# Projection v as seven quarter products, with the block sums of h built from the transposes

## Chip, core and metric

One Trainium2 chip, one of its cores. The metric is the device time of one execution in microseconds (us); the median of three executions is given. The engines run their own queues in order: TensorE (PE in the profile; its weight loads are PEld), VectorE (DVE), ScalarE (ACT), GpSimd (POOL) and SyncE (SP), which here issues the DMAs.

## What is computed

One residual block over 1024 positions of 1024 channels, all in float32:

```python
h    = rmsnorm(x, norm_g)
proj = h @ w_in                     # 1024 x 9216: u, v, z, x_b, c_b, b_b, z_b, g_a, g_b
v    = rmsnorm(gelu(v), v_norm_g)
s    = gelu(u) * (tril(w_s) v + b)  # in chunks of 128 positions
y_a  = s * silu(z)
y_b  = b_b * conv3(c_b * x_b) * silu(z_b)
m    = sigmoid(g_a) * (y_a @ P_a) + sigmoid(g_b) * (y_b @ P_b)
out  = rmsnorm(x + m @ w_out, final_norm_g)
```

The case is about the first part: the norm of x and the projection v, 1024 of the 9216 columns.

## The kernel before

Every float32 product is made of three TensorE matmuls on rounded halves (`mm`, L76): with a = a_hi + a_lo and b likewise, a_hi b_hi + a_lo b_hi + a_hi b_lo. `split` (L72) makes the halves: ACT casts the high one, DVE subtracts it from the source. x is loaded in eight tiles of 128 positions, its squares summed on ACT, the root taken on POOL (`rsqrt_mean`, L60), the tile scaled on DVE, and turned by eight TensorE transposes into two PSUM banks (`transpose_x`, L111). So h lies in four quarters `B[kh][th]` (half kh of the channels, half th of the positions), high and low; DVE copies it once more into `hst`, and it is written to `h_d` in device memory.

All later projections are made in seven quarter products instead of eight (`step`, L331): with B11, B21, B22 the quarters and T1 = B12 - B11, T2 = B22 - T1, T3 = B22 - B12, T4 = B21 - T2, and like sums S1 to S4 of the weight quarters (`weights`, L302). The T blocks are made by `h_blocks` (L272), which reads the quarters back from `h_d` and splits the differences. Projection v alone, the first one, is a plain product: loop L216 makes its left 512 columns, tile by tile as x arrives (`pv0`, 8 x 8 x 3 matmuls of 512 columns), loop L288 its right 512 columns (`pv1`, the same number), with `h_blocks` queued inside it. `v_out` (L129) takes a PSUM bank through Gelu and a square on ACT and writes the tile to `v_d`.

Order: inside `manual_schedule` the named engines keep the order of the code (L142: all five; L215: SP, ACT, DVE); elsewhere a planner orders the instructions. Space: 20 buffers of 8 KB a partition (`big`), ten of 4 KB (`page`: halves of weights, tiles of v), two for raw weights (`rawt`), eight PSUM banks. An allocation waits until a buffer of its kind is free. After v the first step is `pbc0` (`proj("bc", 0)`, L398).

## Time and profile before

| | us |
|---|---|
| median of three executions | 989.87 |
| lowest, highest | 987.47, 991.25 |
| the profiled execution | 991.29 |
| its span, first to last instruction | 989.6 |

Times of rows count from the span's start. An instruction's row has its start, its length, its engine and line, what it writes and reads, and in brackets the idle time ahead of it with what ended it. Matmuls are pipelined: a row of 0.39 us is followed by the next before it ends, so the distance of starts is the cost.

### The profile page before, as it was taken

How to read it: one execution, taken by the hardware profiler on the slowest of the kernel's cores; microseconds unless marked ns; L12 is line 12 of the kernel's file. 1: busy time of each engine (PE TensorE's matmuls, PEld its weight loads, DVE VectorE, ACT ScalarE, POOL GpSimd, SP SyncE). 2: the span in 40 equal slices, each digit the busy share in tenths (PEclk: the TensorE clock that was granted, in tenths of full speed). 3: DMA queues.
4: the chain of work that ended last, by engine and by line, in shares of the span. 5: the costliest groups of instructions: out<-in, count | busy, mean ns of one | idle time of the engine just before them, and what ended most of it. 6: DMA issues, size and time to landing. Idle time of an engine off the chain costs nothing.

```text
span 989.6 us, 10913 instructions
## 1 busy us (share of the span) xinstructions
PE 963.7 (97%) x4310; PEld 796.7 (81%) x4310; DVE 658.4 (67%) x746; ACT 406.4 (41%) x544; POOL 32.3 (3%) x73
## 2 busy tenths in 40 slices
...
GB/s 241 187 144 188 202 144 44 43 137 67 43 117 85 43 118 79 92 154 50 187 98 117 117 86 215 343 338 326 323 243 302 291 286 243 212 373 49 123 106 107
DMA packets 129113, 164.83 MB, mean 167 GB/s; under 512 B 4229, under 2 KB 87205, under 8 KB 125478
## 3 DMA queue, kind: packets, MB, share of 16 engines
...
q10 hardware_dynamic: 576, 1.05, 0.3%
...
q14 instruction: 18, 0.15, 0.0%
...
## 4 chain that ended last, share of the span: by engine, by line
PE 87%; DMA 7%; DVE 2%; ACT 2%; issue 1%; SPq 0%; POOL 0%; POOLq 0%; ACTq 0%; DVEq 0%
PE pbc_x L79 5%; PE pu_x L79 4%; PE pga_x L79 4%; PE pbz_x L79 4%; PE ox L79 4%; PE ax L79 4%; PE pgb_x L79 4%; PE pz_x L79 4%; PE pbb_x L79 4%; PE pbx_x L79 4%; PE bx L79 4%; DMA h<-h_d 3%; PE be L79 2%; PE pbc_e L79 2%; PE oe L79 2%; PE ae L79 2%
## 5 line engine op out<-in xcount | busy, mean ns | idle before, releaser
L79 PE MATMUL pv<-wv_hi,h_hi 128*128 128x512 f32 x120 | 48.2, 402 | 5.6 <-ACT h_hi L73 5.1
L79 PE MATMUL pv<-wv_hi,h_lo 128*128 128x512 f32 x120 | 47.3, 397 | 0.6 <-DVE h_lo L74 0.6
L79 PE MATMUL pv<-wv_lo,h_hi 128*128 128x512 f32 x120 | 47.2, 394 | 0.0
L79 PEld LDWEIGHTS pv<-wv_hi,h_hi 128*128 128x128 f32 x120 | 22.9, 191 | 11.2 <-ACT h_hi L73 5.5
L74 DVE TENSOR_TENSOR yaP_lo<-yaP,yaP_hi 128x1024 fp32r<-128x1024 f32 x14 | 16.9, 1220 | 22.5 <-ACT yaP_hi L73 22.5
L79 PEld LDWEIGHTS pv<-wv_hi,h_lo 128*128 128x128 f32 x120 | 22.9, 191 | 5.6 <-DVE h_lo L74 1.1
L79 PEld LDWEIGHTS pv<-wv_lo,h_hi 128*128 128x128 f32 x120 | 22.9, 191 | 4.9 <-DVE wv_lo L74 0.3
L270 DVE TENSOR_TENSOR h<-h,h 128x1024 f32<-128x1024 f32 x8 | 9.4, 1221 | 21.9 <-DMA h<-h_d 21.9
L338 DVE TENSOR_TENSOR pbz<-pbz_z,pbz 128x512 f32<-128x512 f32 x4 | 2.8, 691 | 28.6 <-PE pbz_z L79 28.6
L74 DVE TENSOR_TENSOR h_lo<-xp,h_hi 128x512 fp32r<-128x512 f32 x16 | 11.0, 685 | 14.5 <-ACT h_hi L73 14.4
L406 DVE SCALAR_TENSOR_TENSOR pbx<-pbc,cwT,pbx 128x1023 f32<-128x1023 f32 (+1 forms) x16 | 20.1, 1276 | 0.0
L74 DVE TENSOR_TENSOR ybP_lo<-ybP,ybP_hi 128x1024 fp32r<-128x1024 f32 x14 | 16.8, 1217 | 4.0 <-ACT ybP_hi L73 4.0
L338 DVE TENSOR_TENSOR pz<-pz_z,pz 128x512 f32<-128x512 f32 x4 | 2.8, 691 | 24.9 <-PE pz_z L79 24.9
L338 DVE TENSOR_TENSOR pbx<-pbx_z,pbx 128x512 f32<-128x512 f32 x4 | 2.8, 692 | 24.9 <-PE pbx_z L79 24.9
L74 DVE TENSOR_TENSOR wv_lo<-wv_raw,wv_hi 128x1024 fp32r<-128x1024 f32 x4 | 4.9, 1223 | 20.1 <-ACT wv_hi L73 20.1
L65 POOL TENSOR_SCALAR ro<-oss4a 128x1 f32<-128x1 f32 x1 | 0.2, 191 | 537.8 <-ACT osq4a L603 537.8
L131 ACT ACTIVATE v<-pv 128x512 f32<-128x512 f32 x16 | 9.5, 596 | 16.8 <-PE pv L79 10.8
L73 ACT CAST yoP_hi<-mt 128x1024 fp32r<-128x1024 f32 x6 | 6.3, 1053 | 22.4 <-DVE mt L270 22.4
L448 PEld LDWEIGHTS pm<-cst,va 128*128 128x128 f32 x128 | 14.9, 192 | 0.3
L448 PE MATMUL pm<-cst,va 128*128 128x128 f32 x128 | 14.9, 275 | 0.0
L73 ACT CAST T_hi<-h 128x1024 fp32r<-128x1024 f32 x8 | 8.4, 1047 | 15.0 <-DVE h L270 14.8
L79 PE MATMUL pbc_x<-h_hi,pbc_ahi 128*128 128x512 f32 x16 | 7.3, 459 | 7.3 <-ACT pbc_ahi L73 7.3
...
## 6 DMA issues: line engine op xcount, KB each, us to landing
...
```

What stands on the lines that cost most here:

```text
L65: nc.gpsimd.tensor_scalar(u, ss, 1.0 / D, t, ALU.mult, ALU.add)
L73: nc.scalar.copy(hi, src)
L74: nc.vector.tensor_tensor(lo, src, hi.bitcast(F32), ALU.subtract)
L79: nc.tensor.matmul(acc, a[i], b[j], start=start and n == 0, stop=stop and n == 2, skip_group_check=not check)
L131: nc.scalar.activation(vt, pv, AF.Gelu)
L270: nc.vector.tensor_tensor(out_[:, js, :], a[:, js, :], b[:, js, :], op)
L338: add = lambda o, a: nc.vector.tensor_tensor(o, a, o, ALU.add)
L406: nc.vector.scalar_tensor_tensor(xx[:, b, t:], c[:, b, :S - t], col(2 - t), xx[:, b, t:], ALU.mult, ALU.add)
L448: nc.tensor.matmul(pm[:, n * P:(n + 1) * P], v[:, b, h * HP + n], wsT[:, gg_ * P:(gg_ + 1) * P], start=True, stop=True)
```

## The change

v becomes seven quarter products P1 to P7 like the other projections, with positions in the role that columns had: A11, A12, A21, A22 are the quarters of its weights (A12 is the lower left, A21 the upper right). P1 = B11 A11 starts as x arrives, tile by tile of 128 positions; P2 = B21 A12 and P5 = T1 S1 follow in the same written order, which now holds all five engines until P5's last matmul. P6, P7, P3 and P4 stand behind it in the planner's part. The results of P1, P6, P7 and P4 add up in four banks `vx`, those of P5 and P3 in four banks `ve`, P2's are added on DVE from `vz`.

`h_d` is gone. `keep` copies the transposes of the first four tiles out of PSUM on ACT, `diff` subtracts these copies from the transposes of the last four on DVE, which gives T1 and T2 as the tiles come; T3 and T4 are one more difference each of what is kept. The B12 quarter has no halves of its own any more. All of x and of v's weights is asked for at the start; A22 is loaded a second time later, since S1 and S2 are made in its place on POOL. The weights of `pbc0` are loaded and split before P4 (`early`), in `big` buffers. The new functions and the order (what is removed stands in the listing above):

```diff
-    B = [[tuple(block4(big(f"h{kh}{th}_{n}", F32R)) for n in ("hi", "lo")) for th in range(2)]
-         for kh in range(2)]
-    h_d = dram("h_d", [P, KT, S])
...
+    BLOCKS = ["B11", "B21", "B22", "T1", "T2", "T4", "T3"]
+    T, raw_h = {}, {}
+    def new_block(n):
+        T[n] = tuple(block4(big(f"{n}_{m}", F32R)) for m in ("hi", "lo"))
...
+    def square_x(i):
...
+        nc.scalar.activation(sq, xs[i], AF.Square, accum_out=ss)
+        rx[i] = rsqrt_mean([ss], f"rx{i}")
+    def norm_x(i):
+        nc.vector.scalar_tensor_tensor(xs[i], xs[i], rx[i], g_bc, ALU.mult, ALU.mult)
...
+    def block_of(i, kh):
+        return ("B11", "B21")[kh] if i < 4 else ("T1", "B22")[kh]
+    def cols(t, i):
+        return t[:, :, i % 4 * P:(i % 4 + 1) * P]
...
+    def transposes(i, kh):
+        n = block_of(i, kh)
+        if i % 4 == 0:
+            new_block(n)
+            n = {"B22": "T2"}.get(n, n)
+            raw_h[n] = block4(big(f"{n}_raw"))
+        p = psum(f"xp{i}_{kh}")
+        for k in range(HP):
+            nc.tensor.transpose(p[:, k * P:(k + 1) * P], xs[i][:, (kh * HP + k) * P:(kh * HP + k + 1) * P], ident)
+        pt[i, kh] = block4(p)
+    def part_src(i, kh):
+        return cols(raw_h["T1"], i) if (i >= 4, kh) == (True, 0) else pt[i, kh]
+    def high(i, kh):
+        nc.scalar.copy(cols(T[block_of(i, kh)][0], i), part_src(i, kh))
+    def low(i, kh):
+        hi, lo = T[block_of(i, kh)]
+        tt(cols(lo, i), part_src(i, kh), cols(hi, i).bitcast(F32), ALU.subtract)
+    def keep(i, kh):
+        nc.scalar.copy(cols(raw_h[block_of(i, kh)], i), pt[i, kh])
+    def diff(i, kh):
+        a, b = (("T1", "B11"), ("T2", "T1"))[kh]
+        tt(cols(raw_h[a], i), pt[i, kh], cols(raw_h[b], i), ALU.subtract)
...
-        for j in range(1, 4):
-            start_rows(j)
+        start_rows(1)
         for i in (2, 3):
             nc.sync.dma_start(xs[i], x[0, i * P:(i + 1) * P, :])
+        for j in (2, 3):
+            start_rows(j)
...
+        for i in (4, 5):
+            xs.append(load_x(i))
+        w_raw = {"A11": raws[0], "A12": raws[1]}
+        def v_raw(n, kh):
+            w_raw[n] = block4(big(f"wv_{n}"))
+            for j in range(2):
+                rows = wv[(kh * HP + 2 * j) * P:(kh * HP + 2 * j + 2) * P, D + NH:2 * D]
+                nc.sync.dma_start(w_raw[n][:, 2 * j:2 * j + 2, :], rows.rearrange("(j p) e -> p j e", p=P))
+        v_raw("A21", 0)
+        for i in (6, 7):
+            xs.append(load_x(i))
+        v_raw("A22", 1)
+        def v_mm(bank, w, t, m, start=True):
+            for k in range(HP):
+                mm(bank, [h[:, k, m * P:(m + 1) * P] for h in T[t]], w[k], start and k == 0, k == HP - 1, start)
+        def v_hi(n, j):
+            hi, lo = (page(f"wv{n}{j}_{m}", F32R).rearrange("p (j e) -> p j e", j=2) for m in ("hi", "lo"))
+            nc.scalar.copy(hi, w_raw[n][:, 2 * j:2 * j + 2, :])
+            return hi, lo
+        def v_lo(n, j, hi, lo, eng=nc.vector):
+            eng.tensor_tensor(lo, w_raw[n][:, 2 * j:2 * j + 2, :], hi.bitcast(F32), ALU.subtract)
+            return [(hi[:, k, :], lo[:, k, :]) for k in range(2)]
+        def v_parts(n):
+            return [w for j in range(2) for w in v_lo(n, j, *v_hi(n, j))]
+        vx, vz, ve, vq = [], [], [], {"C11": block4(big("vC11"))}
+        def p1(m):
+            vx.append(psum(f"vx{m}"))
+            v_mm(vx[m], w0, "B11", m)
+        def p2(m):
+            vz.append(psum(f"vz{m}"))
+            v_mm(vz[m], w2, "B21", m)
+        def p5(m):
+            ve.append(psum(f"ve{m}"))
+            v_mm(ve[m], ws1, "T1", m)
+        def snap(q, m, bank):
+            nc.scalar.copy(vq[q][:, m, :], bank)
+        def add(q, m, bank):
+            o = vq[q][:, m, :]
+            tt(o, bank, o, ALU.add)
+        def first_norm(i, r, h):
+            cs = halves[h]
+            nc.vector.scalar_tensor_tensor(xs[i][:, cs], xs[i][:, cs], r, pg[h], ALU.mult, ALU.mult)
...
         r0 = rsqrt_mean(ss0, "rx0")
-        for h, cs in enumerate(halves):
-            nc.vector.scalar_tensor_tensor(xs[0][:, cs], xs[0][:, cs], r0, pg[h], ALU.mult, ALU.mult)
+        first_norm(0, r0, 0)
+        first_norm(0, r0, 1)
         w0 += start_split(0, nc.gpsimd)
...
+        square_x(1)
+        transposes(0, 0)
+        high(0, 0)
+        low(0, 0)
...
         w0 += start_split(1, nc.gpsimd)
...
+        vx.append(psum("vx0"))
+        for b, a, k in [(0, 0, 0), (0, 0, 1), (0, 1, 0), (0, 1, 1), (1, 0, 0), (1, 0, 1)]:
+            nc.tensor.matmul(vx[0], T["B11"][a][:, k, :P], w0[k][b], start=a + b + k == 0, stop=False)
+        square_x(2)
+        keep(0, 0)
+        transposes(1, 0)
+        high(1, 0)
+        for b, a, k in [(0, 0, 2), (0, 0, 3), (0, 1, 2), (0, 1, 3), (1, 0, 2), (1, 0, 3)]:
+            nc.tensor.matmul(vx[0], T["B11"][a][:, k, :P], w0[k][b], start=False, stop=(b, k) == (1, 3))
         for h, cs in enumerate(halves):
             nc.vector.tensor_copy(g_bc[:, cs], pg[h])
...
+        norm_x(2)
+        low(1, 0)
+        square_x(3)
+        snap("C11", 0, vx[0])
+        transposes(2, 0)
+        high(2, 0)
+        keep(1, 0)
+        norm_x(3)
+        low(2, 0)
+        p1(1)
+        w2 = [v_hi("A12", 0)]
+        square_x(4)
+        w2[0] = v_lo("A12", 0, *w2[0], nc.gpsimd)
+        transposes(3, 0)
+        snap("C11", 1, vx[1])
+        high(3, 0)
+        keep(2, 0)
+        p1(2)
+        w2.append(v_hi("A12", 1))
+        low(3, 0)
+        norm_x(4)
+        w2 = w2[0] + v_lo("A12", 1, *w2[1])
+        transposes(0, 1)
+        high(0, 1)
+        low(0, 1)
+        square_x(5)
+        snap("C11", 2, vx[2])
+        keep(3, 0)
+        p1(3)
+        transposes(1, 1)
+        high(1, 1)
+        keep(0, 1)
+        low(1, 1)
+        norm_x(5)
+        square_x(6)
+        p2(0)
+        snap("C11", 3, vx[3])
+        transposes(2, 1)
+        transposes(4, 0)
+        high(2, 1)
+        keep(1, 1)
+        low(2, 1)
+        diff(4, 0)
+        high(4, 0)
+        s1 = w_raw["S1"] = w_raw["A22"]
+        nc.gpsimd.tensor_tensor(s1[:, :2], w_raw["A21"][:, :2], s1[:, :2], ALU.add)
+        square_x(7)
+        nc.gpsimd.tensor_tensor(s1[:, 2:], w_raw["A21"][:, 2:], s1[:, 2:], ALU.add)
+        add("C11", 0, vz[0])
+        norm_x(6)
+        p2(1)
+        transposes(3, 1)
+        transposes(5, 0)
+        high(3, 1)
+        ws1 = [v_hi("S1", j) for j in range(2)]
+        ws1 = [w for j in range(2) for w in v_lo("S1", j, *ws1[j], nc.gpsimd)]
+        keep(2, 1)
+        low(3, 1)
+        diff(5, 0)
+        low(4, 0)
+        high(5, 0)
+        add("C11", 1, vz[1])
+        norm_x(7)
+        p2(2)
+        transposes(6, 0)
+        keep(3, 1)
+        low(5, 0)
+        diff(6, 0)
+        high(6, 0)
+        add("C11", 2, vz[2])
+        p2(3)
+        transposes(7, 0)
+        low(6, 0)
+        diff(7, 0)
+        high(7, 0)
+        add("C11", 3, vz[3])
+        low(7, 0)
+        transposes(4, 1)
+        high(4, 1)
+        p5(0)
+        low(4, 1)
+        diff(4, 1)
+        transposes(5, 1)
+        high(5, 1)
+        transposes(6, 1)
+        high(6, 1)
+        p5(1)
+        for i in (5, 6):
+            low(i, 1)
+            diff(i, 1)
+        w_raw["S2"] = s1
+        for j in range(2):
+            nc.gpsimd.tensor_tensor(s1[:, 2 * j:2 * j + 2], s1[:, 2 * j:2 * j + 2],
+                                    w_raw["A11"][:, 2 * j:2 * j + 2], ALU.subtract)
+        transposes(7, 1)
+        high(7, 1)
+        low(7, 1)
+        diff(7, 1)
+        new_block("T2")
+        ws2 = []
+        for j in range(2):
+            js = slice(2 * j, 2 * j + 2)
+            split(*(t[:, js, :] for t in T["T2"]), raw_h["T2"][:, js, :])
+            ws2 += v_lo("S2", j, *v_hi("S2", j))
+        for js in (slice(0, 2), slice(2, 4)):
+            tt(w_raw["A21"][:, js], w_raw["A11"][:, js], w_raw["A21"][:, js], ALU.subtract)
+        for js in (slice(0, 2), slice(2, 4)):
+            tt(w_raw["A12"][:, js], w_raw["A12"][:, js], s1[:, js], ALU.subtract)
+        p5(2)
+        p5(3)
...
+    for m in range(HP):
+        v_out(m, 0, vq["C11"][:, m, :])
...
+    def h_parts(n):
+        new_block(n)
         for js in (slice(0, 2), slice(2, 4)):
...
+            split(*(t[:, js, :] for t in T[n]), raw_h[n][:, js, :])
+    def weights(w, c0, name, early=False):
...
         def parts(n, src):
-            hi, lo = (page(f"{name}_{n}{m}", F32R).rearrange("p (k e) -> p k e", k=KT) for m in ("hi", "lo"))
+            if early:
+                t = big(f"{name}_{n}", F32R).rearrange("p (m k e) -> p m k e", m=2, k=KT)
+                hi, lo = t[:, 0], t[:, 1]
+            else:
+                hi, lo = (page(f"{name}_{n}{m}", F32R).rearrange("p (k e) -> p k e", k=KT) for m in ("hi", "lo"))
             split(hi, lo, src)
...
+    def v_prep(p):
+        sub = ALU.subtract
+        if p == "P6":
+            return ws2
+        if p == "P7":
+            tt_halves(raw_h["B11"], raw_h["T2"], raw_h["B11"], sub)
+            raw_h["T3"] = raw_h["B11"]
+            w_raw["S3"] = w_raw["A21"]
+            h_parts("T3")
+            return v_parts("S3")
+        if p == "P3":
+            w_raw["S4"] = w_raw["A12"]
+            return v_parts("S4")
+        v_raw("A22", 1)
+        tt_halves(raw_h["B21"], raw_h["B21"], raw_h["T2"], sub)
+        raw_h["T4"] = raw_h["B21"]
+        h_parts("T4")
+        return v_parts("A22")
...
+    seq = [("P5", "T1"), ("P6", "T2"), ("P7", "T3"), ("P3", "B22"), ("P4", "T4")]
+    wp = ws1
+    for n, (p, t) in enumerate(seq):
+        wn = v_prep(seq[n + 1][0]) if n + 1 < len(seq) else None
+        q = {"P5": "C22", "P6": "C12", "P7": "C22", "P3": "C12"}.get(p)
+        if q and q not in vq:
+            vq[q] = block4(big("v" + q))
+        if p == "P4":
+            first_w = weights(wv, 4 * D, "pbc0", True)
+        for m in range(HP):
+            bank = (ve if p in ("P5", "P3") else vx)[m]
+            if p != "P5":
+                v_mm(bank, wp, t, m, False)
+            if p in ("P5", "P6"):
+                nc.scalar.copy(vq[q][:, m, :], bank)
+            elif p == "P4":
+                v_out(m, 1, bank)
+                v_norms(m)
+            else:
+                o = vq[q][:, m, :]
+                tt(o, bank, o, ALU.add)
+                v_out(m + HP, int(p == "P7"), o)
+                if p == "P3":
+                    v_norms(m + HP)
+        wp = wn
+        if p == "P3":
+            pc = psum("pcw")
+            nc.tensor.transpose(pc[:, :4 * G], cw, ident[:4 * G, :4 * G])
+            nc.vector.tensor_copy(cwT, pc[:, :4 * G])
...
-        c, px = proj("bc", g)
+        c, px = proj("bc", g, None if g else first_w)
```

## Rows read from the trace of the kernel before

**Rows 1.** The page's first part: engine, busy us, share of the span, instructions.

```profile
PE 963.7 (97%) x4310; PEld 796.7 (81%) x4310; DVE 658.4 (67%) x746; ACT 406.4 (41%) x544; POOL 32.3 (3%) x73
```

**Rows 2.** Busy time by stretch: us, each engine, TensorE clock, DMA share, GB/s.

```profile
12.00:14.00 2.00, 2.00 (x6) 1.58 (x5) 2.00 (x5) 2.00 (x3) 1.81 (x3) 0.50 1.04 411
...
18.00:20.00 2.00, 2.00 (x10) 1.65 (x9) 2.00 (x5) 1.98 (x4) 0.48 (x2) 1.00 0.03 7
...
120.00:130.00 10.00, 5.15 (x11) 3.76 (x12) 6.62 (x9) 4.58 (x7) 2.34 (x4) 0.50 0.84 238
...
150.00:250.00 100.00, 100.00 (x443) 82.85 (x442) 66.91 (x79) 36.64 (x46) 0.00 (x0) 1.00 0.24 72
```

**Rows 3.** Timeline of TensorE, 57 to 131 us: start, us, instruction, idle before.

```profile
57.65 0.80 PE L79 MATMUL pv<-wv_hi,h_hi 128*128 128x512 f32 x1 [5.07 <-ACT h_hi L73]
...
62.27 0.40 PE L79 MATMUL pv<-wv_hi,h_hi 128*128 128x512 f32 x1
...
77.04 0.51 PE L79 MATMUL pv<-wv_hi,h_hi 128*128 128x512 f32 x1 [0.55 <-ACT wv_hi L73]
...
124.38 0.79 PE L79 MATMUL pbc_x<-h_hi,pbc_ahi 128*128 128x512 f32 x1 [7.26 <-ACT pbc_ahi L73]
...
130.34 0.39 PE L79 MATMUL pbc_e<-T_hi,pbc_shhi 128*128 128x512 f32 x1
```

**Rows 4.** Waits of 0 to 135 us: total us, times, longest.

```profile
DVE h L270 <- DMA h<-h_d: 21.9, 4, 9.3
...
ACT v L131 <- DMA v_d<-v: 5.7, 3, 2.3
```

**Rows 5.** Timeline of TensorE, 11 to 30 us.

```profile
11.39 1.22 PE L200 MATMUL pv<-wv_hi,h_hi 128*128 128x512 f32 x2 [2.16 <-ACT h_hi L73]
...
24.37 1.03 PE L118 MATMUL xp<-ident,x 128*128 128x128 f32 x8
...
25.16 0.48 PE L79 MATMUL pv<-wv_hi,h_lo 128*128 128x512 f32 x1
...
26.41 0.39 PE L79 MATMUL pv<-wv_hi,h_hi 128*128 128x512 f32 x1
...
29.59 0.39 PE L79 MATMUL pv<-wv_lo,h_hi 128*128 128x512 f32 x1
```

**Rows 6.** Instructions by line and shape, 0 to 145 us: busy us, mean ns, idle before.

```profile
L74 DVE TENSOR_TENSOR h_lo<-xp,h_hi 128x512 fp32r<-128x512 f32 x16 | 11.0, 685 | 14.5 <-ACT h_hi L73 14.4
...
L133 ACT ACTIVATE vsq<-v 128x512 bf16<-128x512 f32 x16 | 10.1, 630 | 0.4
...
L74 DVE TENSOR_TENSOR T_lo<-h,T_hi 128x1024 fp32r<-128x1024 f32 x8 | 9.6, 1223 | 0.5 <-ACT T_hi L73 0.5
...
L131 ACT ACTIVATE v<-pv 128x512 f32<-128x512 f32 x16 | 9.5, 596 | 16.8 <-PE pv L79 10.8 <-DMA v_d<-v 5.7 <-PE pv L200 0.3
...
L73 ACT CAST h_hi<-xp 128x512 fp32r<-128x512 f32 x16 | 8.7, 587 | 11.6 <-PE xp L118 11.6
...
L73 ACT CAST T_hi<-h 128x1024 fp32r<-128x1024 f32 x8 | 8.4, 1047 | 15.0 <-DVE h L270 14.8
...
L107 ACT ACTIVATE sq<-x 128x1024 bf16<-128x1024 f32 x6 | 6.4, 1068 | 0.0
...
L109 DVE SCALAR_TENSOR_TENSOR x<-x,rx3r,gg 128x1024 f32<-128x1024 f32 x1 | 1.3, 1287 | 0.0
```

**Rows 7.** Timeline of POOL, 12 to 88 us.

```profile
12.85 2.39 POOL L161 TENSOR_TENSOR wv_lo<-wv_raw,wv_hi 128x1024 fp32r<-128x1024 f32 x1
...
84.25 0.19 POOL L65 TENSOR_SCALAR rv<-vss 128x1 f32<-128x1 f32 x1
...
86.51 1.09 POOL L65 TENSOR_SCALAR rv<-vss 128x1 f32<-128x1 f32 x1
```

**Rows 8.** Timeline of DVE, 15 to 89 us.

```profile
15.09 2.37 DVE L161 TENSOR_TENSOR wv_lo<-wv_raw,wv_hi 128x1024 fp32r<-128x1024 f32 x2
...
86.33 2.36 DVE L270 TENSOR_TENSOR h<-h,h 128x1024 f32<-128x1024 f32 x2 [5.90 <-DMA h<-h_d]
```

**Rows 9.** Chain of waits in order of time, one write of v.

```profile
29.46 5.28 DMA v_d<-v
```

More of the change, by code (lines that the diff above doesn't have):

```diff
@@ L93, in hybrid_block @@
     rv = const.tile([P, NT], F32, name="rv")
+    tt = nc.vector.tensor_tensor
     x2 = {}
@@ L102, in load_x @@
         return xt
-    def norm_x(i, xt, g):
+    rx, pt = {}, {}
+    def square_x(i):
         sq = small.tile([P, D], BF16, tag="junk", name=f"sq{i}", bufs=1)
         ss = small.tile([P, 1], F32, tag="ss", name=f"ss{i}")
-        nc.scalar.activation(sq, xt, AF.Square, accum_out=ss)
-        r = rsqrt_mean([ss], f"rx{i}")
-        nc.vector.scalar_tensor_tensor(xt, xt, r, g, ALU.mult, ALU.mult)
-    def transpose_x(i, xt):
-        cs = slice(i % 4 * P, (i % 4 + 1) * P)
-        st = page(f"hst{i}").rearrange("p (k t) -> p k t", k=KT)
-        for kh in range(2):
-            pt = psum(f"xp{i}_{kh}")
-            for k in range(HP):
-                ds_ = slice((kh * HP + k) * P, (kh * HP + k + 1) * P)
-                nc.tensor.transpose(pt[:, k * P:(k + 1) * P], xt[:, ds_], ident)
-            src = block4(pt)
-            hi, lo = B[kh][i // 4]
-            split(hi[:, :, cs], lo[:, :, cs], src)
-            nc.vector.tensor_copy(st[:, kh * HP:(kh + 1) * HP, :], src)
-        nc.sync.dma_start(h_d[:, :, i * P:(i + 1) * P], st)
@@ L125, in hk @@
-    def hk(i, k):
-        cs = slice(i % 4 * P, (i % 4 + 1) * P)
-        return [h[:, k % HP, cs] for h in B[k // HP][i // 4]]
+        nc.scalar.activation(sq, xs[i], AF.Square, accum_out=ss)
[6 more added lines that the diff above has]
+        return t[:, :, i % 4 * P:(i % 4 + 1) * P]
@@ L187, in hybrid_block @@
+        first_norm(0, r0, 1)
         w0 += start_split(0, nc.gpsimd)
-        sq1 = small.tile([P, D], BF16, tag="junk", name="sq1", bufs=1)
-        ss1 = small.tile([P, 1], F32, tag="ss", name="ss1")
-        nc.scalar.activation(sq1, xs[1], AF.Square, accum_out=ss1)
-        r1 = rsqrt_mean([ss1], "rx1")
-        transpose_x(0, xs[0])
-        for h, cs in enumerate(halves):
-            nc.vector.scalar_tensor_tensor(xs[1][:, cs], xs[1][:, cs], r1, pg[h], ALU.mult, ALU.mult)
-        w0 += start_split(1, nc.gpsimd)
@@ L196, in hybrid_block @@
-        w0 += start_split(2, nc.vector)
-        pv0 = psum("pv0_0")
-        def first_mm(a, b, k):
-            nc.tensor.matmul(pv0, hk(0, k)[a], w0[k][b], start=a + b + k == 0, stop=b == 1 and k == KT - 1)
-        for a, b, k in [(0, 0, 0), (0, 0, 1), (1, 0, 0), (1, 0, 1), (0, 0, 2), (0, 0, 3), (1, 0, 2), (1, 0, 3)]:
-            first_mm(a, b, k)
-        w0 += start_split(3, nc.vector)
-        transpose_x(1, xs[1])
+        square_x(1)
+        transposes(0, 0)
+        high(0, 0)
+        low(0, 0)
@@ new lines, in hybrid_block @@
+        for h in range(2):
+            first_norm(1, rx[1], h)
+        w0 += start_split(1, nc.gpsimd)
+        vx.append(psum("vx0"))
[7 more added lines that the diff above has]
+            nc.tensor.matmul(vx[0], T["B11"][a][:, k, :P], w0[k][b], start=False, stop=(b, k) == (1, 3))
@@ new lines, in hybrid_block, with tt_halves @@
+        for j in range(2):
[8 more added lines that the diff above has]
+        p5(3)
+    def tt_halves(out_, a, b, op):
+        for js in (slice(0, 2), slice(2, 4)):
+            tt(out_[:, js, :], a[:, js, :], b[:, js, :], op)
@@ L325, in weights, with v_norms @@
         return w_
+    def v_prep(p):
[16 more added lines that the diff above has]
+        return v_parts("A22")
+    def v_norms(i):
+        rsqrt_mean([vss[:, 2 * i + h:2 * i + h + 1] for h in range(2)], f"rv{i}", rv[:, i:i + 1])
+    seq = [("P5", "T1"), ("P6", "T2"), ("P7", "T3"), ("P3", "B22"), ("P4", "T4")]
[27 more added lines that the diff above has]
+            nc.vector.tensor_copy(cwT, pc[:, :4 * G])
     def product(bank, a, b, start, check=True):
@@ L329, in product, with step @@
             mm(bank, [t[:, k, :] for t in a], [t[:, k, :] for t in b], start and k == 0, k == HP - 1, check)
-    def step(w, c0, T, name):
-        w_ = weights(w, c0, name)
+    def step(w, c0, T, name, w_=None):
+        w_ = w_ or weights(w, c0, name)
         C = big(name).rearrange("p (b t) -> p b t", b=2)
```

80 lines of the change are left out of this document (2 added, 78 removed).

## Prediction

> **What bounds the kernel now.** The page comes first: TensorE is busy 97% of the span, so only a change of its work, or of the time in which it has none, moves the end [rows 1]. [...] Whatever comes after the projection v is a full TensorE queue; this change can only move the moment at which that queue begins, and all later work moves with it.
>
> The timeline of TensorE gives that moment and the holes ahead of it [rows 3]. The first step of the next stage (`pbc0`) has its first 12 matmuls at the low clock; the 13th starts at 130.34, and 12 at full speed take 2.72 us (below), so the step begins, in full-speed terms, at 127.62. Two holes stand before it. The wait of 7.26 ahead of 124.38 begins at 117.12; from there to 130.34 are 13.22 us for 2.72 us of work: 10.5 lost. The wait of 5.07 ahead of 57.65 begins at 52.58; nine matmuls (2.04 us) then last until 62.27: 7.65 lost. A third wait of 0.55 follows at 77.04. Sum 18.7 us. The waits say why the long one is there: DVE stood 21.9 us for blocks read back from `h_d` (four waits, the longest 9.3), and the cast of the first `pbc0` weights is queued behind the blocks made of them [rows 4].
>
> **Work taken away.** Before, v takes 8 tiles x 2 halves x 8 k x 3 = 384 matmuls of 512 columns; after, 7 products x 4 x 4 x 3 = 336. Between 26.41 and 29.59 stand 14 of them: 0.227 us each [rows 5]. 48 x 0.227 = 10.9 us. The 64 transposes stay; eight take 0.79 (24.37 to 25.16), four 0.40 [rows 5]. The eight `h_d` writes, six reads and 16 DVE copies into `hst` go. With both holes gone too, the most that can be won is 10.9 + 18.7 = 29.6 us. What the change brings in decides how much of that is kept.
>
> **The new order, first part.** It is one written order for all engines up to the last matmul of P5, so I walked each queue with row durations [rows 6]: ACT 0.59 for a 512-column cast or copy, 1.05 for 1024, 1.07 for a square; DVE 0.69, 1.22 and 1.28 for the norm; POOL 2.39 for 1024 columns [rows 7]. Loads no longer wait for anything: 8.4 MB asked for at once are 20.4 us at the 411 GB/s of 12 to 14 us [rows 2], which with a slower start puts x7 at some 24 us and the last at 27; the walk asks for x7 at 34 and for the last of A22 at 35, so loads that take half as long again would cost it about one microsecond. The start is as before: matmuls from 11.4 at the low clock, full speed from about 17.4 (the 12 to 14 us row has 0.50, the 18 to 20 us row 1.00) [rows 2, 5].
>
> At 17.4 TensorE has left 14 groups of four transposes (5.6 us) and 27 tiles of 12 matmuls (73.5 us): without a wait v would end at 96.5. The walk adds these waits:
> - P1 and the first tile of P2 run to 30.5 with one wait of 0.4: a tile with its transposes takes TensorE 3.1 us, ACT some 2.9 (a square, a cast, two copies), DVE 2.0 (a norm, a low part).
> - PSUM: P1's four banks stay occupied to the end of v, which leaves four for transposes, P2 and P5. P2's second tile waits 1.0 for a bank that `keep(1,1)` reads last (ACT, behind `high(2,1)`), its third 1.8 for one that `diff(5,0)` reads last (DVE, behind `low(3,1)`). Queued behind them on TensorE is everything.
> - P5 needs S1's low half, the fourth of six long POOL operations in a row: 1.2. P5's second tile waits 1.4 for a bank that DVE holds with `low`/`diff`.
> - P6 needs T2 and S2, made after the last transposes: 5.4 us of P5 hide most of four casts and four subtractions; 0.3 and 0.9 are left.
>
> That is 7.0 us, P6 ending at 71.0. Of it 2.9 hang on one thing that the trace of before shows by halves. POOL and DVE exclude each other in one direction: at 86.51 a POOL operation on one column took 1.09 us; the first of two DVE subtractions (2.36 together) with both inputs in SBUF had begun at 86.33, ends near 87.5, and the POOL operation ends at 87.6; another of its line lasts 0.19 [rows 7, 8]. The other direction, a DVE operation that begins while a POOL one runs, the trace has only over 0.15 us at 15.09, where nothing is seen [rows 7, 8]; so its price lies between 0 and the rest of a POOL operation (up to 2.39). I take it as real, because a resource that is handed over whole one way leaves no room for sharing the other way: five DVE operations with two SBUF inputs (norms of x4 and x7, lows of x4, x6, x7) begin inside POOL's and are held 6.1 us in sum, and POOL is held by DVE in turn. Without it P6 ends at 67.9. [...]
>
> **Second part: P7, P3, P4 and the hand-over.** These are three products of 48 matmuls, 10.9 us each. P7 needs T3 and S3. DVE comes out of the written order at 61.3 with four differences still to do (A21, A12: 4.7), then T3's two (2.4), T3's two lows and S3's first (3.6): 72.0 to 73.0, against 71.0 on TensorE. I put 1.5 us for that wait. Then P3 and P4: DVE has some 14 long subtractions (17.1), eight sums (5.5) and the first step's weights (7.1) from 66 to 105, 30 us in 39; ACT has 16 `v_out` of at least 1.23 (19.7), 13 long casts and nine short operations (19), 39 us in 46. Both fit, ACT narrowly. Nothing of `pbc0` but its weights is missing at the end, and those now load and split before P4; so the 10.5 us hole has no reason to return. If ACT's cover is gone, the weight casts come late and each late microsecond is paid whole.
>
> End of v: 96.5 + 7.0 + 1.5 = 105.0, against 127.6: 22.6 us earlier. The profiled execution took 991.29 (its span 989.6), so 968.7 by it; the median of the runs is 989.87, which makes 967.3. I forecast 968.
>
> **Rivals.**
> 1. DVE is not held by POOL: P6 at 67.9, v at 102. 964 to 965. For it: the 0.15 us at 15.09. Chance 0.2.
> 2. The clock falls in the new waits. Waits of 0.55 left it at full (77.04), 5.07 and 7.26 did not [rows 3]; the new ones of 1.0 to 1.8 lie between, and the 2.16 ahead of 11.39, with the low clock behind it, is not far [rows 5]. One fall cost 2.6 us beyond its wait after 57.65 (7.65 - 5.07), 3.2 after 124.38. One or two falls: 971 to 975. Chance 0.18.
> 3. ACT becomes the bound of the second part. At 39 of 46 us, with `v_out` waiting for pages that only a landed write frees (three such waits, 5.7 us, in before [rows 4]), casts for T3, A22 or the first step come 4 to 12 us late: 972 to 980. Chance 0.13. The case that the change does no more than remove 48 matmuls, all holes returning elsewhere, is its far end: 979. Chance 0.01.
> 4. Slower: the same queue, in full. The weights hold eight of ten pages, so `v_out` has two; a write of v took 5.28 us to land [rows 9]. If each of the ten `v_out` from the third to the twelfth stands in ACT's queue for one landing ahead of a cast that TensorE needs, ACT is 52.8 us longer; 7 of that is its slack and 22.6 the gain: 23 us over before, 1013. It decides at (7 + 22.6)/5.28, six such waits. Against it: the second part's order is the planner's, which places an operation when its page is due, and only three waits stood in before. Chance 0.03; at half strength, some six waits, no change, 0.03.
>
> **How the numbers follow.** Forecast 0.42, 968, its own range 965 to 971. Range for 8 in 10: from 962, below the first rival, since the floor is 989.9 - 29.6 = 960.3, to 977, inside the third; left out are some 0.03 below and 0.12 above. A measurement here tells 0.5% (5 us) from no change; the forecast and the first three rivals lie more than 5 us under 989.9 (0.94 with what stands between them); the fourth gives the rest. Faster 0.94, same 0.03, slower 0.03.
>
> **What would show it.** TensorE's timeline: the `pbc0` step begins at 103 to 107 without a wait of several microseconds before it; 336 matmuls of v; no wait on `h_d`. Waits of 1 to 2 us at P2's second and third tile with DVE or ACT readers of a transpose bank as releaser; one at P5's first tile on POOL; one at P6's and P7's first on DVE. For the exclusion: norms or lows of DVE at 24 to 49 us that last, or stand, until a POOL operation ends. Wrong would make it: a clock row of 0.5 after 20 us (rival 2); `v` waiting for `v_d` on ACT with casts behind it (rivals 3, 4); a load landing after 30 us; more than 9 us of waits before P6.

## The result, and the profile after

The changed kernel takes 967.88 us (967.67 to 968.41) against 990.41 (987.47 to 991.25) of the kernel before, run beside it: a ratio of 0.978 (95% interval 0.976 to 0.980), 22.5 us less. The forecast was 968. Its profiled execution took 967.86, its span 966.1. One execution among the runs below took 1608.29 us, at a mean clock of 0.557, and is left out of the times of its run.

The first line of the page answers [rows 1]: TensorE has 48 instructions fewer and 17.1 us less busy time, in which the slower matmuls at before's clock of 0.50 count too. The table of stretches answers [rows 2], its columns again the stretch in us, PE, PEld, DVE, ACT, POOL, clock, DMA share, GB/s.

```profile
PE 946.6 (98%) x4262; PEld 781.9 (81%) x4262; DVE 668.4 (69%) x751; ACT 419.4 (43%) x568; POOL 54.6 (6%) x80
```

```profile
12.00:14.00 2.00, 1.72 (x11) 1.16 (x9) 1.76 (x3) 1.68 (x4) 2.00 (x2) 1.00 1.06 392
...
30.00:40.00 10.00, 7.71 (x41) 6.13 (x40) 7.50 (x9) 6.82 (x11) 8.53 (x7) 1.00 0.01 2
40.00:50.00 10.00, 8.14 (x44) 6.32 (x42) 9.82 (x9) 2.80 (x5) 8.93 (x4) 1.00 0.00 1
...
60.00:70.00 10.00, 10.00 (x45) 8.13 (x44) 9.82 (x9) 9.98 (x21) 0.00 (x0) 1.00 0.54 173
...
120.00:130.00 10.00, 10.00 (x46) 8.29 (x45) 4.16 (x6) 2.28 (x4) 0.00 (x0) 1.00 0.00 0
```

From 120 to 130 us, where TensorE had 5.15 us of work at clock 0.50, it is now full at 1.00. Behind the start, most of what is left of idle time lies between 30 and 60 us; from 40 to 50 DVE is busy 9.82 of 10 and POOL 8.93. TensorE's timeline names every wait (start, us, instruction, idle time before it and its releaser), and answers [rows 3]:

```profile
10.84 0.73 PE L285 MATMUL vx<-wv_hi,B_hi 128*128 128x512 f32 x2 [2.81 <-ACT B_hi L147]
...
16.86 0.66 PE L140 MATMUL xp<-ident,x 128*128 128x128 f32 x4 [1.51 <-DVE x L124]
...
20.08 0.60 PE L140 MATMUL xp<-ident,x 128*128 128x128 f32 x4
...
23.30 0.60 PE L140 MATMUL xp<-ident,x 128*128 128x128 f32 x4
...
31.47 0.50 PE L79 MATMUL vz<-wvA_hi,B_hi 128*128 128x512 f32 x1 [0.72 <-ACT B_raw L154]
...
34.33 1.03 PE L140 MATMUL xp<-ident,x 128*128 128x128 f32 x8
36.92 0.50 PE L79 MATMUL vz<-wvA_hi,B_hi 128*128 128x512 f32 x1 [1.56 <-DVE T_raw L158]
...
44.54 0.65 PE L140 MATMUL xp<-ident,x 128*128 128x128 f32 x4 [0.94 <-DVE T_raw L158]
...
50.82 0.47 PE L79 MATMUL ve<-wvS_hi,T_hi 128*128 128x512 f32 x1 [1.75 <-DVE T_raw L158]
...
71.35 0.50 PE L79 MATMUL vx<-wvS_hi,T_hi 128*128 128x512 f32 x1 [0.65 <-ACT vC L488]
...
104.67 0.61 PE L79 MATMUL pbc_x<-B_hi,pbc_a 128*128 128x512 f32 x2
```

The `pbc0` step begins at 104.67 without a wait, 22.95 us before its 127.62 in full-speed terms; the spans differ by 23.5.

DVE and POOL show the exclusion that the forecast took as real; [rows 7, 8] had it in one direction only. First DVE, then POOL:

```profile
22.22 2.75 DVE L124 SCALAR_TENSOR_TENSOR x<-x,rx4r,gg 128x1024 f32<-128x1024 f32 x1
...
36.79 0.95 DVE L151 TENSOR_TENSOR T_lo<-T_raw,T_hi 128x512 fp32r<-128x512 f32 x1
...
38.26 2.83 DVE L124 SCALAR_TENSOR_TENSOR x<-x,rx7r,gg 128x1024 f32<-128x1024 f32 x1
41.01 2.87 DVE L151 TENSOR_TENSOR T_lo<-T_raw,T_hi 128x512 fp32r<-128x512 f32 x1
43.81 0.68 DVE L158 TENSOR_TENSOR T_raw<-xp,B_raw 128x512 f32<-128x512 f32 x1
...
45.17 1.50 DVE L151 TENSOR_TENSOR T_lo<-T_raw,T_hi 128x512 fp32r<-128x512 f32 x1
...
47.96 1.52 DVE L151 TENSOR_TENSOR T_lo<-T_raw,T_hi 128x512 fp32r<-128x512 f32 x1
```

```profile
37.15 6.19 POOL L241 TENSOR_TENSOR wvS_lo<-wv_A,wvS_hi 128x1024 fp32r<-128x1024 f32 x2
43.30 5.63 POOL L386 TENSOR_TENSOR wv_A<-wv_A,wv_raw 128x1024 f32<-128x1024 f32 x2
```

The norm of x7 takes 2.83 where one alone takes 1.28 [rows 6]; a low part of 512 columns takes 2.87 instead of 0.69 and ends at 43.88, 0.54 after POOL's pair has ended at 43.34. POOL's two pairs take 6.19 and 5.63 instead of 4.8. The difference at 43.81, one of whose inputs lies in a bank, runs its usual 0.68 beside POOL.

### The profile page after: what moved, and what is told of

The parts are those of the page before. It is cut to its first block, busy times and chain, and to the rows that moved or that the text cites. A ratio compares the mean times of both kernels' runs of the same rounds, so it can differ in the third digit from the quotient of the medians.

```text
span 966.1 us, 10828 instructions
## 1 busy us (share of the span) xinstructions
PE 946.6 (98%) x4262; PEld 781.9 (81%) x4262; DVE 668.4 (69%) x751; ACT 419.4 (43%) x568; POOL 54.6 (6%) x80
## 4 chain that ended last, share of the span: by engine, by line
PE 93%; ACT 2%; DVE 2%; POOL 1%; issue 1%; DMA 1%; POOLq 0%; SPq 0%; ACTq 0%
PE pu_x L79 5%; PE pga_x L79 5%; PE pbz_x L79 5%; PE ox L79 5%; PE ax L79 5%; PE pgb_x L79 5%; PE pz_x L79 5%; PE pbb_x L79 5%; PE pbx_x L79 5%; PE pbc_x L79 5%; PE bx L79 4%; PE vx L79 3%; PE be L79 2%; PE oe L79 2%; PE ae L79 2%; PE pgb_e L79 2%
## 5 line engine op out<-in xcount | busy, mean ns | idle before, releaser
L74 DVE TENSOR_TENSOR yaP_lo<-yaP,yaP_hi 128x1024 fp32r<-128x1024 f32 x14 | 16.9, 1221 | 22.5 <-ACT yaP_hi L73 22.5
L151 DVE TENSOR_TENSOR B_lo<-xp,B_hi 128x512 fp32r<-128x512 f32 x12 | 8.2, 684 | 10.7 <-ACT B_hi L147 10.7
L73 ACT CAST yaP_hi<-yaP 128x1024 fp32r<-128x1024 f32 x14 | 14.4, 1048 | 0.0
L73 ACT CAST ybP_hi<-ybP 128x1024 fp32r<-128x1024 f32 x14 | 14.1, 1048 | 0.0
L79 PE MATMUL vx<-wvS_hi,T_hi 128*128 128x512 f32 x32 | 12.6, 394 | 0.6 <-ACT vC L488 0.6
L79 PE MATMUL vx<-wvS_hi,T_lo 128*128 128x512 f32 x32 | 12.5, 391 | 0.0
L140 PEld LDWEIGHTS xp<-ident,x 128*128 128x128 f32 x64 | 7.5, 140 | 6.0 <-DVE x L124 1.9
L616 DVE TENSOR_TENSOR pu<-pu,pz 128x2048 f32<-128x2048 f32 x4 | 9.2, 2291 | 4.4 <-ACT pz L532 4.4
L140 PE MATMUL xp<-ident,x 128*128 128x128 f32 x64 | 9.3, 276 | 2.9 <-DVE x L124 1.5
L79 PE MATMUL vx<-wvS_lo,T_hi 128*128 128x512 f32 x32 | 11.9, 393 | 0.0
L588 DVE TENSOR_TENSOR pbx<-pbx,pbz 128x2048 f32<-128x2048 f32 x4 | 9.2, 2293 | 3.7 <-ACT pbz L532 3.5
```

The costliest lines, as they stand in the source:

```text
L73: nc.scalar.copy(hi, src)
L74: nc.vector.tensor_tensor(lo, src, hi.bitcast(F32), ALU.subtract)
L79: nc.tensor.matmul(acc, a[i], b[j], start=start and n == 0, stop=stop and n == 2, skip_group_check=not check)
L140: nc.tensor.transpose(p[:, k * P:(k + 1) * P], xs[i][:, (kh * HP + k) * P:(kh * HP + k + 1) * P], ident)
L151: tt(cols(lo, i), part_src(i, kh), cols(hi, i).bitcast(F32), ALU.subtract)
L588: nc.vector.tensor_tensor(xx, xx, z, ALU.mult)
```

## Experiments

Times are medians of four executions; the kernel before was run beside each group (988.4 to 990.4).

**The work taken away.** The last product of v is issued twice:

```
             if p != "P5":
                 v_mm(bank, wp, t, m, False)
+                if p == "P4":
+                    v_mm(bank, wp, t, m, False)
```

> The changed kernel with the 48 matmuls of the last product of v (P4) issued twice into the same bank (the last quarter of v is twice its fourth product too much), so that v costs 384 matmuls again; the order before it is untouched. Theory: the stretch has no hole (TensorE busy 10.00 of 10 at clock 1.00), so 48 x 0.227 = 10.9 us come back: 978.8. If the stretch had slack, as when ScalarE set its pace, less: 970 to 975.

Measured: 979.19 (978.75 to 979.48), 11.3 more than the changed kernel. The 48 added matmuls are paid in full where they stand, so the term 10.9 holds.

**The exclusion, taken away.** Left out are the long POOL operations behind the first weights (sums S1 and S2, the lows of S1 and of half of w2):

```
-        w2[0] = v_lo("A12", 0, *w2[0], nc.gpsimd)
-        nc.gpsimd.tensor_tensor(s1[:, :2], w_raw["A21"][:, :2], s1[:, :2], ALU.add)
-        nc.gpsimd.tensor_tensor(s1[:, 2:], w_raw["A21"][:, 2:], s1[:, 2:], ALU.add)
...
```

> The changed kernel without the long GpSimd operations after the first weights: the low part of half of w2, the sums S1 and S2 and the low parts of S1 are left out (those operands take the high part or the raw block, so v is wrong in its low digits and blocks). Theory of the exclusion: five VectorE operations no longer stand 6 to 7 us behind GpSimd, and the end of the fifth product's stretch comes 2.6 to 2.9 us earlier: 965.0 to 965.3. If VectorE was late for another reason (its own queue, banks), no change: 967.9. If GpSimd's chain also held the weights of P2 and P5, up to 4 us: 964.

Measured: 964.43 (964.19 to 964.94), 3.4 less, somewhat more than the 2.6 to 2.9 of the theory. DVE's low part that took 2.87 takes 0.69, the two waits at 44.54 and 50.82 are gone, and 40 to 60 us are full (DVE's timeline, then the table of stretches):

```profile
39.24 0.69 DVE L151 TENSOR_TENSOR T_lo<-T_raw,T_hi 128x512 fp32r<-128x512 f32 x1
```

```profile
40.00:50.00 10.00, 10.00 (x56) 8.49 (x54) 7.22 (x12) 2.80 (x5) 0.00 (x0) 1.00 0.00 0
50.00:60.00 10.00, 10.00 (x48) 8.09 (x47) 8.84 (x10) 7.69 (x10) 0.00 (x0) 1.00 0.01 2
```

The waits at 31 and 37 stay (0.73 and 1.56): those two are banks, not POOL. The edit also takes away POOL's own chain, but that did not hold P5: undisturbed, S1's two low parts would have ended at 41.95 (from 37.15, 2.4 each), and P5's first matmul starts at 43.87 here. So the price of the exclusion is the two waits of P5, 0.94 and 1.75 by the rows, 3.4 by the time.

**The two bank waits.** The operations that free the banks go first:

```
+        keep(1, 1)
         high(2, 1)
-        keep(1, 1)
...
+        diff(5, 0)
         low(3, 1)
-        diff(5, 0)
```

> The changed kernel with two pairs of statements exchanged: keep(1,1) ahead of high(2,1) on ScalarE and diff(5,0) ahead of low(3,1) on VectorE, so that the banks of the second and the third tile of P2 come free earlier. If each wait of TensorE is paid for in full, 0.7 of the 0.72 and 0.85 of the 1.56 go: 967.9 - 1.6 = 966.3. Rival: the stretch from 30 to 60 is set by VectorE's queue and its exclusion with GpSimd, and what is gained at 31 and 37 comes back as waits at 44 to 51: 967.9 (967.4 to 968.2).

Measured: 967.50 (three executions, 967.45 to 967.96): no change, as the rival had it. TensorE's timeline shows the gain made and given back, DVE's why:

```profile
34.88 0.47 PE L79 MATMUL vz<-wvA_hi,B_hi 128*128 128x512 f32 x1 [0.88 <-DVE T_raw L158]
...
38.48 0.66 PE L140 MATMUL xp<-ident,x 128*128 128x128 f32 x4 [0.62 <-ACT B_raw L154]
...
44.17 0.66 PE L140 MATMUL xp<-ident,x 128*128 128x128 f32 x4 [1.82 <-DVE T_raw L158]
...
50.44 0.47 PE L79 MATMUL ve<-wvS_hi,T_hi 128*128 128x512 f32 x1 [0.19 <-DVE T_raw L158]
```

```profile
34.04 0.69 DVE L158 TENSOR_TENSOR T_raw<-xp,B_raw 128x512 f32<-128x512 f32 x1 [0.35 <-PE xp L140]
...
35.24 2.17 DVE L151 TENSOR_TENSOR T_lo<-T_raw,T_hi 128x512 fp32r<-128x512 f32 x1
37.33 0.68 DVE L266 TENSOR_TENSOR vC<-vz,vC 128x512 f32<-128x512 f32 x1
```

The wait at P2's second tile is gone, that at its third is 0.88 instead of 1.56, and TensorE comes to the third tile 2.0 us earlier (34.88 for 36.92; 0.36 of it is an earlier start of this execution). But the low part behind them now meets POOL and takes 2.17 where it took 0.95, so DVE comes to its next sum at 37.33 against 37.66: no more than the earlier start. P5's second tile begins at 50.44 against 50.82, the same 0.4. In between the clock fell (mean 0.50 from 46 to 48 us) and cost nothing: the low clock stands in the place of the wait of 1.75. Whoever sets the pace here is DVE behind POOL; a wait ahead of it is not worth what its row says.

**ScalarE at the hand-over to P7.** The four outputs of v's first quarter are written after P6:

```
-    for m in range(HP):
-        v_out(m, 0, vq["C11"][:, m, :])
...
+        if p == "P6":
+            for m in range(HP):
+                v_out(m, 0, vq["C11"][:, m, :])
```

> The changed kernel with the four outputs of the first quarter of v (gelu, square, store) written after the products P5 and P6 instead of ahead of them: ScalarE, busy 9.98 of 10 from 60 to 70, has 1.28 of table load and 5 us of outputs less there, and copies P6's last bank sooner. If the wait of 0.65 ahead of P7 is ScalarE's copy and nothing else is late behind it: 967.2. Rival: P7's own weights or the outputs in P7 and P3 are then late instead: 967.9 to 969.

Measured: 966.53 (966.15 to 966.93), 1.35 less. The wait ahead of P7 is gone, and `pbc0` begins at 103.00. Of the 1.67 by which that is earlier, 0.66 are an earlier start of this execution (P2's third tile at 36.26 against 36.92), so 1.0 is the edit's in the profile.

**The weights of the next stage.** The early load is taken out:

```
-        if p == "P4":
-            first_w = weights(wv, 4 * D, "pbc0", True)
```

> The changed kernel without the early weights: the first step of the next stage loads and splits its weights in its own place, into pages, as in the kernel before; v itself is untouched. The prediction costed this part at nothing because the last product of v hides it. Theory: without it the raw buffer is free only after P3's weights, and the page, load (4 to 5.4 us) and splits (some 7 us on VectorE) end behind P4: a hole of 2 to 8 us ahead of the first step, 970 to 976. Rival: the loads start early anyway, since the buffers are free and SyncE idle: 967.9.

Measured: 972.38 (971.68 to 972.66), 4.5 more. In TensorE's timeline a cast and a low part stand between P4 and the step, and then the clock falls (mean 0.89 from 100 to 110 us, 0.94 from 110 to 120; a matmul's row is 0.63 instead of 0.39):

```profile
105.74 0.50 PE L79 MATMUL pbc_x<-B_hi,pbc_ahi 128*128 128x512 f32 x1 [1.62 <-ACT pbc_ahi L73]
107.00 0.50 PE L79 MATMUL pbc_x<-B_hi,pbc_alo 128*128 128x512 f32 x1 [0.76 <-DVE pbc_alo L74]
...
108.69 0.63 PE L79 MATMUL pbc_x<-B_hi,pbc_ahi 128*128 128x512 f32 x1
```

**How much of the gain needs the seven products?** These runs start from the kernel before, with its 384 matmuls. First all loads at the start (x4 to x7, then v's second weights into buffers of their own), the trip through memory kept:

```
+        for i in (4, 5, 6, 7):
+            xs.append(load_x(i))
+        raw1 = []
+        for k in (0, 4):
+            raw1.append(block4(big(f"wv1{k}_raw")))
+            nc.sync.dma_start(raw1[-1], wv[k * P:(k + 4) * P, ...])
         r0 = rsqrt_mean(ss0, "rx0")
```

> The kernel before, with x4 to x7 and both halves of v's second weights asked for at the start, the weights into big buffers of their own instead of the two raw ones; nothing else is changed, the 384 matmuls stay. Theory of the prediction (the first hole, 7.65 us ahead of 57.65, is a late load behind stores in SP's queue): it goes, 990.4 - 7.65 = 982.7 at most. If the second hole (10.5 us ahead of 124.38) is mainly the two raw buffers handed from load to load since the second weights' load at 68.92, and not the trip through memory itself, the first of the block loads starts some 9 us earlier and that hole nearly goes too: 973 to 975. If the trip to memory makes the second hole, it stays: 982 to 983.

Measured: 982.8 (981.9 to 984.88), 6.4 less. Both holes are small now, but a new one stands at the first tile (chain of waits; ScalarE; TensorE):

```profile
16.67 11.12 DMA h_d<-hst
```

```profile
27.87 1.28 ACT L131 ACT_TABLE_LOAD   x1 [11.40 <-DMA h_d<-hst]
```

```profile
31.04 0.79 PE L79 MATMUL pv<-wv_hi,h_hi 128*128 128x512 f32 x1 [6.45 <-ACT h_hi L73]
```

A store asked for behind the loads lands 11.12 us later and holds a page, which ScalarE's gelu needs. In the next run the block loads read x, and in the one after it the stores and their copies are left out as well:

```
-        nc.sync.dma_start(t, h_d[:, kh * HP:(kh + 1) * HP, halves[th]])
+        nc.sync.dma_start(t, x[0, kh * NH:(kh + 1) * NH, halves[th]].rearrange(...))
...
-            nc.vector.tensor_copy(st[:, kh * HP:(kh + 1) * HP, :], src)
-        nc.sync.dma_start(h_d[:, :, i * P:(i + 1) * P], st)
```

> As the run with the early loads, and the six block loads read x instead of the stored transposes (the sums of blocks are of other data, so the output of all that follows is other; shapes, queues and bytes are the same): nothing waits for a store of the transposes. Both holes gone: 990.4 - 18.7 = 971.7, the most that the kernel before could gain without the seven products. Against it the changed kernel (967.9) would then show what the seven products bring net: 10.9 less the 7.0 us of new waits, 3.9 us. If holes are left, 973 to 977.

> The kernel before with the early loads and the block loads reading x, and now without the copies of the transposes (16 on VectorE) and their 8 stores (the sums of blocks are of other data, as before). In the run with the early loads the first store, asked for at 16.67 behind the loads, landed 11.12 us later and held a page, and with it the gelu at 27.84: the hole of 6.5 us moved from 57.65 to the start of tile 1. If that is why the early loads brought 6.4 instead of 17, it goes here: 983.4 - 6.1 = 977.3, and with the smaller holes behind it (2.0 and 2.4) down to 973. The least that two closed holes leave is 989.2 - 18.7 = 970.5. Rival: the early loads themselves crowd the start (tile 1 waits for its rows of weights): the hole stays, 982 to 983.

Measured: 983.36 and 985.18, both misses (971.7 to 977 was expected of the first, 973 to 977.3 or, by the rival, 982 to 983 of the second), and they don't answer the question. Loads that wait for no store are asked for at the very start: in the second run the first subtraction of blocks stood in DVE's queue ahead of tile 1's low part, behind a load of 13.30 us (18.82 to 32.12), and TensorE waited 8.6 us for it. The clean form is to ask early for nothing but v's second weights, in tile 2:

```
+            if i == 2:
+                raw1 = []
+                for k in (0, 4):
+                    raw1.append(block4(big(f"wv1{k}_raw")))
+                    nc.sync.dma_start(raw1[-1], wv[k * P:(k + 4) * P, ...])
...
-                raw = block4(rawt(f"wv1{i}_raw"))
+                raw = raw1[k // 4]
```

> The kernel before with one thing changed: the two loads of v's second weights (1 MB each) are asked for together in tile 2 and into two big buffers of their own, instead of in tiles 4 and 6 into the two raw buffers that the block loads need next. The trip of the transposes through memory, its stores and its reads stay. Nothing stands ahead of the first stores, as it did when all loads were asked for at the start. Theory: both holes are the hand-over of the two raw buffers and ScalarE's queue behind a late load, not the trip itself: the hole of 7.65 goes, and the chain of six block loads starts some 16 us earlier than 80.46 while TensorE is 7.65 earlier, so 1 to 2 of the 10.5 stay: 989 - 7.65 - 9 = 972 to 973. Rival: the trip to memory makes the second hole: 981 to 982. Against 967.9 the first value would leave 4 to 5 us to the seven products and the sums on chip, the second 13 to 14.

Measured: 977.86 (977.54 to 978.85), 10.5 less than its 988.37: between the 972 to 973 of the theory and the 981 to 982 of the rival. The hole ahead of 57.65 has become 2.75 with a clock of 0.83 behind it (50 to 60 us), the long one 1.62 and 0.76:

```profile
49.27 0.50 PE L79 MATMUL pv<-wv_hi,h_lo 128*128 128x512 f32 x1 [2.75 <-DVE h_lo L74]
...
112.42 0.50 PE L79 MATMUL pbc_x<-h_hi,pbc_ahi 128*128 128x512 f32 x1 [1.62 <-ACT pbc_ahi L73]
113.68 0.50 PE L79 MATMUL pbc_x<-h_hi,pbc_alo 128*128 128x512 f32 x1 [0.76 <-DVE pbc_alo L74]
```

Those last two are, to the digit, the waits of the changed kernel without its early weights; but the clock stays at 1.00 behind them here (110 to 120 us), and fell there. What is left of the first hole is the trip's: DVE stood 5.3 for the page of a store of the transposes that had not landed, ahead of the low part that TensorE waited for. The edit asks earlier and also frees the raw buffers; it does not tell the two apart. Last, the early weights of `pbc0` added to this:

```
         if i == 4:
             h_blocks(1)
+        if i == 5:
+            first_w = weights(wv, 4 * D, "pbc0", True)
```

> The kernel before with the early second weights of v (as in the last run of that kind) and, with them, the first step's weights of the next stage loaded and split in the second half of v, as the changed kernel does; 384 matmuls and the trip through memory stay. Taking the early weights out of the changed kernel cost 4.5, so if the parts add up: 977.9 - 4.5 = 973.4, and what the seven products and the sums on chip bring net of their waits is 973.4 - 967.9 = 5.5 of their 10.9. Rival: in this order the weights come late anyway (raw buffers, ScalarE's queue in v's second half) and stand in the way of the blocks: 977 to 980.

Measured: 979.70 (979.02 to 982.65) beside a before of 990.42: no gain (ratio 0.991, without them 0.989). The chain of waits says why: the block loads start when the last store of the transposes has landed (63.32 + 3.52 = 66.84), still follow one another through the two raw buffers, and the weights' load comes behind them.

```profile
63.32 3.52 DMA h_d<-hst
66.86 6.06 DMA h<-h_d
...
94.23 6.83 DMA h<-h_d
...
105.49 5.30 DMA pbc_raw<-in_w_in_dram
```

So a gain of 988.37 - 967.88 = 20.5 us splits in this order: 10.5 for asking earlier for v's second weights, which the kernel before could have had; 5.5 (977.86 - 972.38, both beside the same runs of before) for the seven products with sums on chip, net of their waits; 4.5 for early weights, which brought nothing while the blocks passed through memory and the raw buffers. The parts are good to 1 or 2 us only: 967.88 comes from a group whose before was 990.41, and the fall of the clock at the hand-over is in 972.38's profile and not in 977.86's (from the end of v to the step at full speed, 4.4 us are lost there and 3.3 here).

**An order written around the exclusion.** The same operations up to P5 in another order, the outputs after P6. The aim was that DVE's operations with a bank among their inputs stand beside POOL's long ones, long norms and lows between them, and that what frees a bank goes first. A stretch of it, the statements of all four engines in one order:

```
        transposes(3, 1)
        root_x(6)
        transposes(4, 0)
        high(3, 1)
        p2(1)
        norm_x(6)
        snap("C11", 0, vx[0])
        keep(2, 1)
        add("C11", 0, vz[0])
        s1 = w_raw["S1"] = w_raw["A22"]
        nc.gpsimd.tensor_tensor(s1[:, :2], w_raw["A21"][:, :2], s1[:, :2], ALU.add)
        snap("C11", 1, vx[1])
        high(2, 1)
        diff(4, 0)
        square_x(7)
        low(2, 1)
        transposes(5, 0)
        p2(2)
        diff(5, 0)
        nc.gpsimd.tensor_tensor(s1[:, 2:], w_raw["A21"][:, 2:], s1[:, 2:], ALU.add)
```

In the first of the two runs the two halves of w2 stood exchanged, so P2 multiplied other rows, in the same number and shape; the second also has 18 extra transposes in the idle stretches of the start:

> The changed kernel with the same operations in another order on the four engines up to P5: transposes further ahead of their products, the bank-freeing copies and differences first, the short VectorE operations (one operand from a bank) beside GpSimd's long ones and the long norms and lows between them; the outputs of the first quarter after P6. Bookkeeping with the durations of the trace puts the end of P6 5 to 7 us earlier, and the wait ahead of P7 goes: 961 to 963. If the exclusion alone was the price (the run without the long GpSimd operations gave 3.5), 964.4. Rival: other waits take their place (more banks held, weights' low parts late): 965 to 968.

> The order of the previous reordered run, with two changes: 9 extra transposes of the identity into a bank of their own in each of its two idle stretches at the start (ahead of 9.87 and ahead of 12.73), and the four parts of w2 in their right order. In that run one execution had a mean clock of 0.998 and 961.6 us, three had 0.995 and 964.3 to 965.1. Theory: the difference is a fall of the clock at the start, which this order has no slack to hide, and with TensorE busy there the clock stays: 961.5 to 962.5 in every execution. Rival: the fall is not tied to these idle stretches, or the extra work costs what it saves: 964 to 965.

Measured: 964.49 (961.57 to 965.10), then 962.99 (961.80 to 964.05), 4.9 less than the changed kernel; the ratio to before is 0.974 (0.972 to 0.976) for its 0.978. This beats both kernels. TensorE's waits from 15 to 100 us sum to 1.8. The exclusion is met in part only: POOL's S2 sums take their plain time, but DVE's norm of x6 takes 3.33 and one low part 2.86, 4.2 us of holding for the 7.1 of the changed kernel, and the longest wait left, 1.43, is for a bank that the sum behind that low part frees (TensorE, POOL, DVE):

```profile
41.17 0.50 PE L79 MATMUL vz<-wvA_hi,B_hi 128*128 128x512 f32 x1 [1.43 <-DVE vC L272]
...
100.20 0.62 PE L79 MATMUL pbc_x<-B_hi,pbc_a 128*128 128x512 f32 x2
```

```profile
42.72 2.40 POOL L409 TENSOR_TENSOR wv_A<-wv_A,wv_raw 128x1024 f32<-128x1024 f32 x1
45.06 2.43 POOL L420 TENSOR_TENSOR wv_A<-wv_A,wv_raw 128x1024 f32<-128x1024 f32 x1
```

```profile
27.76 3.33 DVE L127 SCALAR_TENSOR_TENSOR x<-x,rx6r,gg 128x1024 f32<-128x1024 f32 x1
...
37.65 2.86 DVE L154 TENSOR_TENSOR T_lo<-T_raw,T_hi 128x512 fp32r<-128x512 f32 x1
40.44 0.68 DVE L272 TENSOR_TENSOR vC<-vz,vC 128x512 f32<-128x512 f32 x1
```

How much of the 4.9 comes from less holding, and how much from transposes that stand further ahead of their products, no run takes apart; the later outputs alone gave 1.35.

The 18 extra transposes did not hold the clock: in the profiled execution of the second run it was 0.50 from 12 to 14 us, so that half of the theory fell. Whether they make a fall rarer is open.

## Why the forecast held, step by step

- **Work away.** 10.9 forecast; 48 matmuls more cost 11.3.
- **Holes.** 18.7 forecast to close. They closed: nothing of 5.07 or 7.26 is left. Why they stood there was read half right. The forecast blamed the trip through `h_d` for the long one; the runs show the two raw buffers, handed from v's second weights to six block loads to the next weights, as the larger part: moving those two loads alone shrank both holes, 10.5 in sum, with the trip still in place. The trip counts through those buffers, through its stores' pages, and through the last store, which the block loads wait for.
- **Start.** This step was wrong. It was to run at the lower clock, 0.50, until 17.4; it ran at 1.00, and won only 0.5 by it, for the third tile's transposes waited 1.51 for the norm, behind POOL's low parts of the first weights (rx2 at 14.93, behind a `wv_lo` that ended at 14.57). At 16.86 TensorE had left what the forecast gave it at 17.4. Where the clock did fall in the same start (0.50 from 12 to 14 us in the run with late outputs), that wait was 0.55 and the tile began at 16.15.
- **Waits of the new order.** 7.0 forecast, P6's end at 71.0 (the forecast's own terms give 70.8); it ended at 70.70 (71.35 less the 0.65). But the waits by the rows are 5.0, not 7.0: what filled the rest stands below under the sum. The sizes: P2's second and third tiles 1.0 and 1.8, measured 0.72 and 1.56, with the releasers named. P5's first tile 1.2, measured 0.94, but the releaser was misnamed: not S1's low on POOL, but a bank ahead of the transposes before it, held by DVE, which POOL held. P5's second tile 1.4, measured 1.75. P6 0.3 and 0.9, measured nothing.
- **Exclusion.** It had 2.9 of the forecast; taking POOL's long operations away gave 3.4. DVE was held 7.1 us in sum (two norms 1.5 each, low parts 0.3, 2.2, 0.8 and 0.8), forecast 6.1; the low part held longest, by 2.2, is that of x5, which was not among the forecast's five. The first rival, 964 to 965, is what that run gave (964.4). No row of before shows the second direction; the forecast took it from the first by an argument. The trace of the changed kernel shows both, 2.87 for a DVE operation of 0.69 and 6.19 for two POOL operations of 2.4. The difference with an input in a bank kept its 0.68 beside POOL.
- **P7.** 1.5 forecast, with DVE late; measured 0.65, with ScalarE late at P6's banks. The term was mis-sized and misnamed. DVE was as late as forecast: S3's first low part, expected at 72.0 to 73.0, ended at 73.22, 1.9 behind P7's first matmul. But the planner had put matmuls that need only the high weights first, and the first that reads the low part starts at 73.38 (rows below: DVE, then TensorE). The pages of `v_out`, rivals 3 and 4, cost one wait of 2.8 us on ScalarE that TensorE did not feel; ScalarE was near its bound from 60 to 80 us only (9.98 and 9.69 of 10).

```profile
72.00 1.22 DVE L241 TENSOR_TENSOR wvS_lo<-wv_A,wvS_hi 128x1024 fp32r<-128x1024 f32 x1
```

```profile
73.38 0.39 PE L79 MATMUL vx<-wvS_lo,T_hi 128*128 128x512 f32 x1
```

- **Hand-over.** Costed at nothing under P4: right, and worth 4.5 when uncovered. v ends at 104.67, forecast 105.0.

The sum came out within 0.12 us, closer than its terms were, and that is luck. The start (0.5), the waits up to P6 (2.0) and P7 (0.85) all came out under the forecast, 3.4 in sum. What made up for them is a term that the forecast put at nothing: from 16.86 to 104.67 are 87.8 us, less 5.6 of waits 82.2, for work that it priced at 79.1 (5.6 for the transposes, 73.5 for the tiles), so 3.1 more. By the rows a tile with its four transposes takes 3.22 (20.08 to 23.30) where the forecast has 3.12, and eight transposes with a wait behind them take 1.03 (34.33 to 35.36) instead of 0.79.
